# Moving the projection of the embeddings to the start of a two-block kernel on one Trainium2 core

## The chip, the core and the metric

The kernel runs on one core of one Trainium2 chip, as one program. The metric is device time in microseconds (us); less is better. Five engines work side by side, each through its own list of instructions in order: PE (matrix products), ACT (ScalarE), DVE (VectorE), POOL (GpSimd) and SP, which here only issues transfers. Two instructions on different engines are ordered by semaphores alone. The order on each engine is fixed when the program is built: the kernel writes it out by hand.

## What is computed

Two transformer blocks, one after the other, on 256 rows of 1024 numbers in float32. The first is modulated by a condition `c`; the second adds, at its very end, a gated projection of per-row embeddings `p`:

```python
x = x + g1 * (mixed @ w_out)                    # end of the first block's attention
h2 = rms(x, ln2_g) * (1 + sc2) + sh2            # its second norm
x = x + g2 * ((silu(h2 @ w_gate) * (h2 @ w_up)) @ w_down)
...                                             # second block: mixers, feed forward
gate = sigmoid(rms_norm(x, norm_ple_g) @ w_ple_gate)
x = x + gate * (p @ w_ple_proj)                 # p: 256 x 256, w_ple_proj: 256 x 1024
return rms_norm(x, norm_final_g)
```

The product `p @ w_ple_proj` depends on no other result. It may be computed at any time before the last step.

## The kernel before, in words

Rows are cut into two tiles of 128 (`t` = 0, 1). Every weight arrives as a unit of 128 x 2048 float32 (1.05 MB; the units `ko` are 128 x 1536). ACT rounds a unit to `wh`, DVE subtracts to get the rest `wl` (`split`, L281), and each product is made of three matmuls (`mm3`, L449): high by high, low by high, high by low. `_order()` (L50) lists the units in the order in which SP loads them and in which they are split. `load_to` (L265) issues the loads: a unit lies in one of three `raw` buffers (the modulation weights `a1` in slabs of 128 x 1024 instead), and up to four split units (`wh`, `wl`) are alive at a time.

The start, up to L629, is written out by hand. SP issues `pf`, then `a1` unit 0, `x`, `ko` unit 0, and further units (L424 to L432). PE passes its time with dummy products on a tile of ones (`keep_warm`, L552, counts in `WARM`). Then comes `a1` unit 0 (L530: four products on PE, four column scalings on DVE, sum `r`), the sum of squares of both row tiles on ACT (`sumsq`, L514), the reciprocal root on POOL (`rsqrt`, L458), the scaled rows `xn`, their transposes, and `modulate` and `modulate2` (L576, L592), which give the first normed tile `h1b`. From L605 a loop over eight steps multiplies by `ko`: in each step 18 matmuls `pa`, the next `a1` unit and the next modulation.

From L1122 on a planner decides the order: a model of the engines' clocks (`Pace`) is carried along while the program is built, side tasks (`run`) are advanced in `tick` (L396) when the model holds their inputs ready, and `until` (L410) lets the model's PE clock run on while nothing is ready. It sets the order of instructions, not their times on the chip.

The projection of the embeddings is such a side task. `ple_prep` (L1145) loads `p` transposed (tile `pT`, 128 x 512) through POOL's queue and splits it. `ple_proj` (L1153) makes, for each row tile and each half of the columns, six matmuls of 512 columns into `ppa` and copies them by ACT to `ppo`; POOL's queue writes `ppo` to a buffer `pp` in HBM, from where it is read back at the very end (L1688). Its unit `("pp",)` stands behind the units of the first output projection `wo1`, and the condition `spare` (L1295) lets it run only once `wo1` is issued and the planner is idle: that is while the residual and the norm `n2` behind `wo1` (`norm_shift`, L1230, `shift_steps`, L1250) are being worked out for the feed forward step `up`.

Of the kernel before, what the change touches and what calls it, by code (L numbers as in the profile page):

```python
# [10 lines left out]
F32 = mybir.dt.float32  # L11
F32R = mybir.dt.float32r
# [36 lines left out]

def _order():  # L50

    o = [("a1", 0)]
    for j in range(KT):
        o.append(("ko", j))
        if j + 1 < KT:
            o.append(("a1", j + 1))
    ad = lambda s: [("ad", s, q, h) for q in range(2) for h in range(2)]
    m = [(n, u) for n in ("dk", "fv", "dv") for u in range(2)] + [("wo1", h, cb) for h in range(2) for cb in range(2)]
    m.append(("pp",))
    a = ad(0) + ad(1) + ad(2)  # L60
    for i, p in reversed(list(enumerate(ORDER))):
        m[p:p] = a[2 * i:2 * i + 2]
    o += m

    def ffn(n, nb, nd):
        gu = lambda b: [("g" + n, b, 0), ("g" + n, b, 1)]
        dn = lambda b: [("d" + n, b, h) for h in range(nd)]
        r = gu(0) + gu(1)
        for b in range(2, nb):
            r += dn(b - 2) + gu(b)  # L70
        return r + dn(nb - 2) + dn(nb - 1)
    f = ffn("1", NB1, 1)
    for i, k in enumerate(ad(3)):
        f.insert(12 + 4 * i, k)
    o += f
    for hf in range(2):
        for n in ("v", "q", "k"):
            o += [(n, hf, 0), (n, hf, 1)]
    for n in ("zv", "zu", "ga", "gb"):
        for hf in range(2):  # L80
            o += [(n, hf, 0), (n, hf, 1)]
    o += [("wo2", h, cb) for h in range(2) for cb in range(2)]
    o += ffn("2", NB2, 2)
    o += [("pg", hf, h) for hf in range(2) for h in range(2)]
    return o
# [3 lines left out]

A1_FIRST, WARM = True, (20, 4, 4, 2)

ON_DVE = ()
ORDER = (3, 6, 6, 8, 9, 11)
# [111 lines left out]
def body(ctx, tc, ins, out):  # L207
# [20 lines left out]
    def psB(name):  # L228
        if st["paced"]:
            bfree.sort()  # L230
            clock["PE"] = max(clock["PE"], bfree.pop(0))
        return ps.tile([P, 512], F32, tag="B", name=name)
# [4 lines left out]
    def slab(name, dt=F32):  # L237
        return sb.tile([P, 1024], dt, tag="s", bufs=12, name=name)

    def half(name, dt=F32):  # L240
        return sb.tile([P, 512], dt, tag="w", bufs=11, name=name)
# [23 lines left out]
    def load_to(n):  # L265
        while st["dma"] < min(n, len(order)):
            i = st["dma"]
            if order[i][0] == "a1":
                raws[i] = [slab(f"raw{i}{g}") for g in range(2)]
                for g in (1, 0):  # L270
                    Q.dma_start(raws[i][g], src[i][0][:, g * 1024:(g + 1) * 1024])
            else:
                raw = sb.tile([P, 2048], F32, tag="raw", bufs=NRAW, name=f"raw{i}")
                ring.append(raw.tensor.name)
                if len(ring) > NRAW:
                    clock["DMA"] = max(clock["DMA"], pace.last.get(ring[-1 - NRAW], 0.0))
                Q.dma_start(raw[:, :src[i][1]], src[i][0])
                raws[i] = raw
            st["dma"] += 1

# [8 lines left out]
    def process():  # L289

        i, k = st["proc"], order[st["proc"]]
        if st["part"] == 0:
            st["parts"] = par(HALVES) if st["paced"] and not pe_only() else 1
        n, c = st["parts"], st["part"]
        w = src[i][1] // n
        if k[0] in ("a1", "ad"):
            handlers[k[0]](k, raws[i], c)
        else:
            if c == 0:
                assert len(live) < NSP, (k, live)  # L300
                parts[k] = [sb.tile([P, 2048], F32R, tag=q, bufs=NSP, name=f"{q}{i}") for q in ("wh", "wl")]
                live.append(k)
            if st["first"]:
                for a in range(0, w, 512):
                    split(*parts[k], raws[i], a, a + 512)
                    if a == 0:
                        st["first"]()
            else:
                split(*parts[k], raws[i], c * w, (c + 1) * w)
        st["part"] += 1  # L310
        if st["part"] == n:
            raws.pop(i)
            st["part"] = 0
            st["proc"] += 1
            load_to(st["proc"] + (NRAW + 2 if st["proc"] < 13 else NRAW))

    def can_process():
        if st["proc"] == len(order):
# [6 lines left out]
    def use(k, ahead=False, h=1, first=None):  # L325
        st["first"] = first
        while place[k] > st["proc"] or (place[k] == st["proc"] and st["part"] <= h):
            process()
        if not ahead:
            st["used"] = max(st["used"], place[k])  # L330
        return parts[k]
# [20 lines left out]
    def on(*aps, slack=None):  # L352
        return lambda: pace.when(*aps) <= clock["PE"] + (par(SLACK) if slack is None else slack)
# [5 lines left out]
    def slot(n=1):  # L359
        return lambda: sum(f <= clock["PE"] + par(SLACK) for f in bfree) >= n  # L360

    def flag(*names):
        return lambda: all(n in flags for n in names)
# [58 lines left out]

    pf = sb.tile([P, PF_W], F32, name="pf")
    Q.dma_start(pf, ins["pf"])  # L424
    if A1_FIRST:
        load_to(1)
    x = []
    for t in range(NT):
        xt = sb.tile([P, D], F32, name=f"x{t}")
        Q.dma_start(xt, ins["x"][t * P:(t + 1) * P, :])  # L430
        x.append(xt)
    load_to(NRAW)  # L432
    pc = sb.tile([P, PC_W], F32, name="pc")
    bias_t = sb.tile([P, 4096], F32, tag="bias", name="bias1")
    al = bias_t[:, 0:1280].rearrange("p (h k) -> p h k", k=256)
# [13 lines left out]
    def mm3(acc, a, b, start, stop):  # L449
        (ah, al_), (bh, bl) = a, b  # L450
        T.matmul(acc, lhsT=ah, rhs=bh, start=start, stop=False)
        T.matmul(acc, lhsT=al_, rhs=bh, start=False, stop=False)
        T.matmul(acc, lhsT=ah, rhs=bl, start=False, stop=stop)
# [98 lines left out]
    def keep_warm(n):  # L552
        for _ in range(n):
            T.matmul(warm[:, 0:P], lhsT=ones, rhs=ones, start=True, stop=True)

    keep_warm(WARM[0])
    xn1, rx = [], []
    if A1_FIRST:
        process()
    for t in range(NT):  # L560
        ss = sumsq(x[t], f"n1{t}")
        rx.append(rsqrt(ss, 1, 1.0 / D, f"n1{t}"))
        xn1.append(slab(f"xn1{t}"))
    if not A1_FIRST:
        process()
    keep_warm(WARM[1])

    def scale_x(t, a, b):
# [36 lines left out]
    for j in range(KT):  # L605
        wh, wl = use(("ko", j))
        for p in range(3):
            for cb in range(3):
                c = slice(cb * 512, cb * 512 + 512)
                for t in range(NT):  # L610
                    T.matmul(accs[cb][t], lhsT=hT[t][p // 2][:, j, :], rhs=(wh, wl, wh)[p][:, c],
                             start=j == 0 and p == 0, stop=j == KT - 1 and p == 2)
            if p == 0 and j + 1 < KT:
                process()
            if p == 1 and j + 1 < KT:
                modulate(j + 1)
                use(("ko", j + 1))
                modulate2(j + 1)
            if p == 0 and j + 1 == KT:
                use(("dk", 0), True)  # L620
            if p == 0 and j + 1 == KT:
                V.tensor_copy(fgh, pcs("fgw"))
                V.tensor_tensor(fgl, pcs("fgw"), fgh.bitcast(F32), op=ALU.subtract)
        live.remove(("ko", j))
        if j == 4:
            Q.dma_start(pc, ins["pc"])
        if j == 6:
            Q.dma_start(bias_t[:, 0:1280], ins["alibi"])
    use(("dk", 1), True)  # L629


# [506 lines left out]
    proj(("dv",), keep(lambda t: vv[t][:, 512:1024], "dv"))  # L1138


    pp = dr.tile([NT, P, D], F32, name="pp")
    pTh = half("pTh", F32R)
    pTl = half("pTl", F32R)

    def ple_prep():  # L1145
        pT = half("pT")
        G.dma_start(pT, ins["p2T"])
        yield on(pT)
        V.tensor_copy(pTh, pT)
        V.tensor_tensor(pTl, pT, pTh.bitcast(F32), op=ALU.subtract)  # L1150
        flags.add("pT")

    def ple_proj():  # L1153
        for t in range(NT):
            o_ = slab(f"ppo{t}")
            for cb in range(2):
                yield flag("pT"), lambda: ("pp",) in parts, spare, slot()
                acc = psB(f"ppa{t}{cb}")
                wh, wl = use(("pp",))
                for k in range(2):  # L1160
                    o = k * 1024 + cb * 512
                    a = slice(k * 256 + t * P, k * 256 + t * P + P)
                    mm3(acc, (pTh[:, a], pTl[:, a]), (wh[:, o:o + 512], wl[:, o:o + 512]), k == 0, k == 1)
                yield on(acc)
                S.activation(o_[:, cb * 512:(cb + 1) * 512], acc, AF.Copy)
                free(acc)
            G.dma_start(pp[t], o_)
        done(("pp",))


    def out_proj(name, mTs, mflag, fin):
        acc = {}
        for h in range(2):
# [118 lines left out]

        until(flag(f"{nflag}{t}{u}"), on(hTn[t][0][:, 4 * u:4 * u + 4, :], hTn[t][1][:, 4 * u:4 * u + 4, :]))

    def spare():  # L1295
        return st["idle"] and "wo1" in flags

    run(ple_prep())
    run(ple_proj(), 2)
    hT_n, *hT_all = hT_tiles("n2")  # L1300
    out_proj("wo1", mT, "mT", residual(0, norm_shift("n2", hT_n, "n2")))
    hT = hT_n
# [598 lines left out]
```

## Time and profile before

| | |
|---|---|
| three runs | 786.50, 786.51, 786.88 us (median 786.51) |
| the profiled execution, its own time | 787.08 us |
| its span, first to last instruction | 785.3 us |
| PE busy | 770.6 us, 98% of the span |
| DVE, ACT, POOL busy | 66%, 54%, 4% of the span |
| HBM read and written | 156.8 MB and 2.1 MB, 202 GB/s over the span |
| granted TensorE clock, mean | 0.998 |

Times within the trace count from the first instruction. A row of the time line gives start, duration, engine, line, operation, output and inputs, and in brackets how long the engine stood idle before and what it waited for. Every instruction bears L153, the line of the helper that records them; tiles are told apart by name. PEld is the loading of PE's stationary operand. A matmul's duration contains the drain, so successive matmuls overlap; their rate is read from start to start.

### The profile page before, as it was taken

The page shows a single profiled execution, that of the slowest core. Times are in us where ns is not written, and L with a number is a line of the kernel's source. Part 1 is how long each engine was busy: PE and PEld are TensorE (multiplying, and loading weights), DVE is VectorE, ACT ScalarE, POOL GpSimd, SP SyncE. Part 2 cuts the span into 40 slices and gives each one's busy share as a digit, 9 for nine tenths or more (in the row PEclk, how much of TensorE's full clock was granted, in tenths as well). Part 3 has the DMA queues.
Part 4 walks back from the last instruction along what each step waited for, and adds up shares of the span by engine and source line. Part 5 has one row for each costly group of instructions (what it writes and reads, how often), then busy time and mean ns, then how long its engine had stood idle before and what let it go on. Part 6 is the DMA issues. An engine that isn't in the chain of part 4 may idle for free.

```text
span 785.3 us, 10687 instructions
## 1 busy us (share of the span) xinstructions
PE 770.6 (98%) x4110; PEld 631.6 (80%) x4110; DVE 520.4 (66%) x913; ACT 424.9 (54%) x711; POOL 34.4 (4%) x73
## 2 busy tenths in 40 slices
PE   8999999999999999999999999999999999999996
PEld 7777667778888888888879878888888888888885
DVE  4878867667576866558674658746676665566583
ACT  4457467466554554456556584554475455445463
POOL 0000000121100000001100001000010000000011
PEclk9999999999999999999999999999999999999999
DMA  8967853755855666534762334545555544554331
GB/s 338 413 245 300 291 192 126 285 220 193 321 214 215 240 230 227 199 124 159 297 214 68 148 108 161 215 167 209 187 174 203 190 162 184 214 214 183 138 108 54
DMA packets 25251, 159.61 MB, mean 203 GB/s; under 512 B 2944, under 2 KB 3104, under 8 KB 8816
## 3 DMA queue, kind: packets, MB, share of 16 engines
q1 hardware_dynamic: 23184, 152.27, 52.0%
q0 software_dynamic: 2016, 6.66, 2.5%
q8 instruction: 32, 0.52, 0.3%
q14 instruction: 19, 0.16, 0.1%
HBM read 156.80 MB, written 2.12 MB: 202 GB/s over the span
## 4 chain that ended last, share of the span: by engine, by line
PE 91%; ACT 3%; DVE 3%; issue 1%; DMA 1%; POOL 0%; SPq 0%; POOLq 0%; ACTq 0%; DVEq 0%
PE up L153 27%; PE dn L153 19%; PE wo L153 5%; PE pa L153 3%; PE pga L153 3%; PE gb L153 3%; PE ga L153 3%; PE zu L153 3%; PE v L153 2%; PE zv L153 2%; PE dk L153 1%; PE k0T L153 1%; PE q0T L153 1%; PE q1T L153 1%; PE ap L153 1%; PE k1T L153 1%
## 5 line engine op out<-in xcount | busy, mean ns | idle before, releaser
L153 DVE TENSOR_TENSOR wl<-raw,wh 128x1024 fp32r<-128x1024 f32 (+3 forms) x218 | 278.7, 1309 | 109.0 <-ACT wh L153 108.9
L153 ACT ACTIVATE wh<-raw 128x1024 fp32r<-128x1024 f32 (+3 forms) x218 | 235.8, 1124 | 66.2 <-PE up L153 14.2
L153 PE MATMUL up<-n2b,wh 128*128 128x512 f32 x320 | 114.4, 401 | 0.0
L153 PE MATMUL up<-n2b,wl 128*128 128x256 f32 x320 | 89.8, 281 | 0.0
L153 PE MATMUL dn<-wh,aTh 128*128 128x512 f32 x216 | 84.9, 393 | 0.0
L153 PE MATMUL dn<-wl,aTh 128*128 128x512 f32 x216 | 84.3, 390 | 0.0
L153 PE MATMUL dn<-wh,aTl 128*128 128x512 f32 x216 | 84.1, 390 | 0.0
L153 PE MATMUL up<-n4b,wh 128*128 128x512 f32 x224 | 79.5, 399 | 0.0
L153 PEld LDWEIGHTS up<-n2b,wh 128*128 128x128 f32 x320 | 60.1, 188 | 15.6 <-issue 1.1
L153 ACT ACTIVATE fs<-up 128x256 f32<-128x256 f32 x68 | 25.9, 381 | 83.9 <-PE up L153 83.9
L153 PE MATMUL up<-n4b,wl 128*128 128x256 f32 x224 | 62.9, 281 | 0.0
L153 PEld LDWEIGHTS up<-n2b,wl 128*128 128x128 f32 x320 | 60.4, 189 | 1.0 <-issue 0.5
L153 DVE TENSOR_TENSOR fs<-up,fs 128x256 f32<-128x256 f32 x68 | 28.7, 422 | 39.7 <-ACT fs L153 39.5
L153 PEld LDWEIGHTS up<-n4b,wh 128*128 128x128 f32 x224 | 42.1, 188 | 10.3
L153 PEld LDWEIGHTS dn<-wl,aTh 128*128 128x128 f32 x216 | 40.6, 188 | 8.9
L153 PEld LDWEIGHTS dn<-wh,aTh 128*128 128x128 f32 x216 | 40.6, 188 | 8.5
L153 PEld LDWEIGHTS dn<-wh,aTl 128*128 128x128 f32 x216 | 40.6, 188 | 7.9
L153 PEld LDWEIGHTS up<-n4b,wl 128*128 128x128 f32 x224 | 42.3, 189 | 0.3
L153 ACT ACTIVATE aTh<-fs 128x512 fp32r<-128x512 f32 x24 | 15.2, 632 | 37.4 <-DVE fs L153 37.4
L153 DVE TENSOR_TENSOR aTl<-fs,aTh 128x512 fp32r<-128x512 f32 x24 | 16.6, 693 | 16.6 <-ACT aTh L153 16.5
L153 PE MATMUL pa<-wh,h1b 128*128 128x512 f32 x96 | 24.5, 400 | 0.8 <-ACT h1b L153 0.6
L153 PE MATMUL v<-wh,n3b 128*128 128x512 f32 x64 | 20.9, 405 | 0.6 <-DVE n3b L153 0.6
(686 smaller groups left out, 1393.5 us busy)
## 6 DMA issues: line engine op xcount, KB each, us to landing
raw<-in_ws_dram SPq DMA_DIRECT2D x112, 1024.0 KB, 4.8
raw<-in_ada_dram SPq DMA_DIRECT2D x16, 1024.0 KB, 5.0
raw<-in_ada_dram SPq DMA_DIRECT2D x16, 512.0 KB, 10.9
raw<-in_wko_dram SPq DMA_DIRECT2D x8, 768.0 KB, 9.6
bias<-rd POOLq DMA_DIRECT2D x1, 2048.0 KB, 10.7
x<-in_x_dram SPq DMA_DIRECT2D x2, 512.0 KB, 7.2
pp<-ppo POOLq DMA_DIRECT2D x2, 512.0 KB, 3.6
ppt<-pp POOLq DMA_DIRECT2D x2, 512.0 KB, 3.9
```

The lines of the kernel that those rows point to most:

```text
L153: r = f(*a, **k)
```

## The change

The unit `("pp",)` becomes the first of the order. `p` transposed and this unit (in two halves, one transfer each) are loaded right behind `pf`; then `x`; then the modulation and `ko` units. The products are issued behind the first dummy products and ahead of `a1` unit 0, in four accumulators at once, the four copies by ACT stand ahead of the two sums of squares, and the two writes to HBM are issued by POOL in the text behind the `ko` loop. The side tasks are gone from behind `wo1`.

```diff
-    o = [("a1", 0)]
+    o = [("pp",), ("a1", 0)]
...
-    m.append(("pp",))
...
-                Q.dma_start(raw[:, :src[i][1]], src[i][0])
+                w = 1024 if order[i][0] == "pp" else src[i][1]
+                for a in range(0, src[i][1], w):
+                    Q.dma_start(raw[:, a:a + w], src[i][0][:, a:a + w])
...
-            load_to(st["proc"] + (NRAW + 2 if st["proc"] < 13 else NRAW))
+            load_to(st["proc"] + (NRAW + 2 if st["proc"] < 14 else NRAW))
...
-    if A1_FIRST:
-        load_to(1)
+    pT = half("pT")
+    Q.dma_start(pT, ins["p2T"])
+    load_to(1)
     x = []
     for t in range(NT):
         xt = sb.tile([P, D], F32, name=f"x{t}")
         Q.dma_start(xt, ins["x"][t * P:(t + 1) * P, :])
         x.append(xt)
-    load_to(NRAW)
+    load_to(NRAW + 1)
...
     keep_warm(WARM[0])
+
+    pp = dr.tile([NT, P, D], F32, name="pp")
+    pTh = half("pTh", F32R)
+    pTl = half("pTl", F32R)
+    V.tensor_copy(pTh, pT)
+    V.tensor_tensor(pTl, pT, pTh.bitcast(F32), op=ALU.subtract)
+    wh, wl = use(("pp",), first=lambda: None)
+    ppo = [slab(f"ppo{t}") for t in range(NT)]
+    ppa = [[psA(f"ppa{t}{cb}") for cb in range(2)] for t in range(NT)]
+    for k in range(2):
+        for cb in range(2):
+            o = k * 1024 + cb * 512
+            for t in range(NT):
+                a = slice(k * 256 + t * P, k * 256 + t * P + P)
+                mm3(ppa[t][cb], (pTh[:, a], pTl[:, a]), (wh[:, o:o + 512], wl[:, o:o + 512]), k == 0, k == 1)
+    done(("pp",))
     xn1, rx = [], []
-    if A1_FIRST:
-        process()
+    process()
+    for t in range(NT):
+        for cb in range(2):
+            S.activation(ppo[t][:, cb * 512:(cb + 1) * 512], ppa[t][cb], AF.Copy)
     for t in range(NT):
         ss = sumsq(x[t], f"n1{t}")
...
+    for t in range(NT):
+        G.dma_start(pp[t], ppo[t])
     use(("dk", 1), True)
...
-    def ple_proj():
-        for t in range(NT):
-            o_ = slab(f"ppo{t}")
-            for cb in range(2):
-                yield flag("pT"), lambda: ("pp",) in parts, spare, slot()
...
-    run(ple_prep())
-    run(ple_proj(), 2)
```

## Rows read from the trace of the kernel before

**Rows 1.** The page, part 4: shares of the chain that ended last, by engine.

```profile
PE 91%; ACT 3%; DVE 3%; issue 1%; DMA 1%; POOL 0%; SPq 0%; POOLq 0%; ACTq 0%; DVEq 0%
```

**Rows 2.** Busy us by window: PE, PEld, DVE, ACT, POOL, granted clock, DMA share, GB/s.

```profile
5.00:10.00 5.00, 5.00 (x40) 4.47 (x39) 2.23 (x5) 1.06 (x2) 0.00 (x0) 1.00 1.02 417
20.00:30.00 10.00, 10.00 (x60) 7.13 (x58) 8.19 (x16) 4.73 (x6) 0.45 (x1) 1.00 1.02 414
```

**Rows 3.** Time line, the first 14 us: start, duration, engine, operation, [idle before].

```profile
1.04 7.48 PE L153 MATMUL warm<-ones 128*128 128x128 f32 x40 [1.04 <-DVE ones L153]
...
6.37 0.35 DVE L153 TENSOR_SCALAR r<-raw,cond 128x256 f32<-128x256 f32 x1 [3.21 <-DMA raw<-in_ada_dram]
...
8.94 1.06 ACT L153 ACTIVATE n10j<-x 128x1024 f32<-128x1024 f32 x1 [6.06 <-DMA x<-in_x_dram]
...
10.21 1.06 ACT L153 ACTIVATE n11j<-x 128x1024 f32<-128x1024 f32 x1
...
12.11 0.63 ACT L153 ACTIVATE wh<-raw 128x512 fp32r<-128x512 f32 x1 [0.74 <-DMA raw<-in_wko_dram]
...
13.41 0.56 ACT L153 ACTIVATE h1b<-pt,sh,sc 128x256 fp32r<-128x256 f32 x1 [0.68 <-DVE sc L153]
...
14.03 0.74 PE L153 MATMUL pa<-wh,h1b 128*128 128x512 f32 x2 [0.59 <-ACT h1b L153]
```

**Rows 4.** Time line, two steps of the loop over `ko`.

```profile
22.11 0.64 PE L153 MATMUL ap<-raw,condz 128*32 128x256 f32 x8
...
22.60 1.49 ACT L153 ACTIVATE wh<-raw 128x1536 fp32r<-128x1536 f32 x1 [1.87 <-DMA raw<-in_wko_dram]
...
27.68 0.64 PE L153 MATMUL ap<-raw,condz 128*32 128x256 f32 x8
```

**Rows 5.** By tile, `ppa` and `pT`: count, duration min/median/max, first and last start.

```profile
L153 PE MATMUL ppa<-wh,pTh x8: 389/389/499, 166.3 to 172.9; 128*128 128x512 f32 x8
...
L153 ACT ACTIVATE ppo<-ppa x4: 575/588/594, 170.1 to 176.0; 128x512 f32<-128x512 f32 x4
...
L153 DVE CAST pTh<-pT x1: 416/416/416, 146.6 to 146.6; 128x512 fp32r<-128x512 f32 x1
```

**Rows 6.** Time line behind the output projection `wo1`, PE only.

```profile
166.32 0.39 PE L153 MATMUL ppa<-wh,pTh 128*128 128x512 f32 x1
...
168.82 0.39 PE L153 MATMUL ppa<-wl,pTh 128*128 128x512 f32 x1
...
169.65 1.27 PE L153 MATMUL n2t<-pf,n2x 128*128 128x128 f32 x8 [0.45 <-ACT n2x L153]
...
173.37 0.39 PE L153 MATMUL ppa<-wl,pTh 128*128 128x512 f32 x1
```

**Rows 7.** The chain of waits in order of time: start, duration, what it spent.

```profile
160.61 3.02 issue
163.63 0.10 ACT wh L153
163.72 1.73 issue
165.45 0.71 ACT n2j L153 x2
...
170.21 0.92 ACT ppo L153 x2
...
173.84 0.49 ACT ppo L153
...
176.26 7.53 PE up L153 x33
```

**Rows 8.** Time line, the last matmul of the kernel.

```profile
777.24 0.28 PE L153 MATMUL pga<-wl,n5b 128*128 128x256 f32 x1
```

**Rows 9.** By window, columns as in rows 2: the dummy products, and the end.

```profile
1.00:7.00 6.00, 5.96 (x28) 5.96 (x29) 1.10 (x5) 1.21 (x2) 0.00 (x0) 1.00 0.82 255
7.00:8.00 1.00, 1.00 (x11) 1.00 (x10) 0.93 (x3) 0.00 (x0) 0.00 (x0) 1.00 1.01 414
...
782.00:783.00 1.00, 0.00 (x0) 0.00 (x0) 0.00 (x0) 0.00 (x0) 0.00 (x0) 0.50 0.92 348
```

More of the change, by code (lines that the diff above doesn't have):

```diff
@@ L85, in _order @@
     return o
-A1_FIRST, WARM = True, (20, 4, 4, 2)
+WARM = (20, 4, 4, 2)
 ON_DVE = ()
@@ L563, in body @@
         xn1.append(slab(f"xn1{t}"))
-    if not A1_FIRST:
-        process()
     keep_warm(WARM[1])
@@ L1138, in body @@
     proj(("dv",), keep(lambda t: vv[t][:, 512:1024], "dv"))
[L1141 to L1151, printed above, removed]
-    def ple_proj():
-        for t in range(NT):
-            o_ = slab(f"ppo{t}")
-            for cb in range(2):
-                yield flag("pT"), lambda: ("pp",) in parts, spare, slot()
[L1158 to L1168, printed above, removed]
     def out_proj(name, mTs, mflag, fin):
@@ L1293, in halves @@
         until(flag(f"{nflag}{t}{u}"), on(hTn[t][0][:, 4 * u:4 * u + 4, :], hTn[t][1][:, 4 * u:4 * u + 4, :]))
-    def spare():
-        return st["idle"] and "wo1" in flags
-    run(ple_prep())
-    run(ple_proj(), 2)
     hT_n, *hT_all = hT_tiles("n2")
```

## The prediction

> **What bounds the kernel now.** I read four views, in this order. First the shares of the chain that ended last: 91% of it is PE [rows 1], so only what delays PE, or what PE waits for, moves the time. The question is then where PE works on the embeddings' projection now, where it will, and what PE would have done at either place. Second, the time line behind the output projection `wo1` [rows 6] with the chain of waits there [rows 7]: the projection's matmuls start at 166.32 and the last starts at 173.37, but none of them is in the chain. The chain of that stretch runs over ACT: a weight split that waits 3.02 us, the sums of squares `n2j` behind it, and the copies `ppo` (0.92 and 0.49 us), until PE takes `up` without a break from 176.26. So PE fills with the projection a stretch in which it would have to wait anyway. Third, the time line of the first 14 us [rows 3]: PE runs dummy products until 8.52, and the first real matmul `pa` starts at 14.03; its path is x landing, `n10j` at 8.94, `n11j` at 10.21, the roots, the transposes, `h1b` at 13.41. Fourth, the DMA of that stretch: it moves 417 and 414 GB/s at a full share [rows 2], so the start is bounded by bytes and by that path together, while the loop behind it repeats every 27.68 - 22.11 = 5.57 us on PE [rows 4].
>
> **The change, part by part.** The sum is made on the profiled execution: span 785.3, own time 787.08, that is 1.78 us outside the span, which the change doesn't touch. Its own time lies 0.57 us above the median 786.51; I take the difference found and put it on the median.
>
> *The load.* `pT` (128 x 512 x 4 bytes = 0.26 MB) and the unit (1.05 MB) go ahead of all but `pf`: 1.31 MB at 0.417 MB per us [rows 2] = 3.1 us later for every `a1` and `ko` unit. Behind the loop's beginning this is hidden if PE is at least as late (below). x comes ahead of `a1` unit 0 now: ahead of it stand 1.31 MB more and 1.05 MB less, so it lands 0.6 us later than 8.94, at about 9.6; `a1`'s first half, used at 6.37 before [rows 3], has 2.36 MB more ahead of it and comes 5.7 us later, at 12.0.
>
> *The products at the start.* 24 matmuls. From 166.32 to 168.82 eleven intervals take 2.50 us [rows 6], 0.227 us each; 24 of them take 5.45 us, the last one's result standing 0.16 us later than that (its duration is 0.39 [rows 5]). They start when the dummy products end, 8.52, if the first half of the unit has been split by then. Its bytes are `pf`, `pT` and 0.52 MB, 0.26 MB more than `pf` and the first half of `a1` had, which was used at 6.37: so it lands at 7.0, its first quarter is rounded by 7.7 (0.63 us for 128 x 512 [rows 3]), and there is 0.8 us of slack; `pTh` takes 0.42 us [rows 5] before that. So PE ends them at 8.52 + 5.45 + 0.16 = 14.1. Bounds: no later unless the halves land over 0.8 us late; I allow 1.5 us upward, nothing downward, since the number of dummy products stays.
>
> *The copies.* Four on ACT, 0.588 us long [rows 5]; three can follow the accumulators as they finish, the last waits for the last matmul at 14.1, and as the two copies of [rows 7] hold the chain 0.46 us each and more for the first, the next ACT instruction starts some 0.55 us behind: 14.7. That next instruction is `n10j`. Here is the point: in the text the copies stand ahead of the sums of squares, ACT keeps its order, so x, landed at 9.6, waits until 14.7. `n10j` moves from 8.94 to 14.7, by 5.75 us, and the path from it to `pa`, 14.03 - 8.94 = 5.09 us, is unchanged: `a1` unit 0 (12.0, four DVE steps and the sum, about 15 with its products on PE behind the projection's) and `ko` unit 0 (12.11 + 3.1 = 15.2, when ACT is busy with `n11j` until 17.2) both come in time. First `pa`: 14.03 + 5.75 = 19.8. Everything that PE does from there on is 5.75 us later.
>
> *Does the loop stay PE's?* Its loads come 3.1 us later and their consumers 5.75 us, so they gain 2.65 us of margin. Against it stand the two writes of `ppo`, 1.05 MB: POOL has nothing of length between the roots and these writes, so it issues them at about 18 us, into the full DMA: 2.5 us at 0.417 MB per us. The margin covers them. Without it the cost would be up to 2.5 us, since ACT waited 1.87 us for one `ko` unit already [rows 4]; I take 0 and keep 0 to 1.
>
> *What is removed behind `wo1`.* The 24 matmuls leave a hole rather than a gain: the chain there [rows 7] has no `ppa`. What leaves the chain are the copies: 0.92 + 0.49 = 1.4 us. The split with its wait of 3.02 us stays as I read the planner: four split units are alive, so the next split needs the release of `wo1`'s third unit whichever unit it is, and it is emitted at the same point, ahead of `n2j`. A unit is loaded and split one place sooner, but PE doesn't wait for splits in this stretch. Next late behind the copies is the same ACT chain, and at the second tile's transposes PE. Bounds of this gain: 1.4 up to 3.5 (if `n2j` also comes ahead of the split of 163.63 to 165.45 [rows 7]). I take 1.4.
>
> *The rest.* `pT`'s load on POOL's queue at 140, two DVE steps at 147, one split of some 2 us on either engine at 149 leave stretches in which PE is full; that work was hidden, and is worth 0 (its cover is PE's own work, and the planner may order its neighbours a little differently: plus or minus 0.5).
>
> Sum: +5.75 - 1.4 = +4.35 us. 786.51 + 4.35 = 790.9.
>
> **A rule against the trace.** In the hole PE has, from its last `wo` matmul at about 166.5, only eight transposes at 169.65 and three matmuls until about 175. At the end of the kernel the clock reads 0.50 in the window 782 to 783, the lower of the two levels (1.2 against 2.4 GHz), after the last matmul ended at 777.52 [rows 8, 9]; and 28 dummy products took the first 6 us while 11 took the next one [rows 9], so beginning from rest PE is slower too, though the column reads 1.00 there. The Trainium skill, "TensorE: Matmul & The Clock Gate", section "Why this matters for your kernels", warns of idle gaps between bursts of matmuls, since one brings the clock back to its lower level; by it the removed filler would have been what kept the clock up. The trace before has no such hole to test it; this is the second rival.
>
> **The rivals.**
>
> 1. *The hole closes, not slower.* If the planner, without the unit, puts the split elsewhere and `n2j` comes as x is ready, PE could go from `wo` to `up` with no wait. It would gain the 5.45 us and the waits that are there already (0.45 us at 169.65 and a few tenths more [rows 6]), about 6.2 us; against +5.75 that is 786.1. It decides at one place: the first `n2t` must start at 166.6 instead of 169.65, so 3 us must leave the chain ahead of it, and of those only the split's 1.8 us are in sight [rows 7]. With the start at its lower bound, the bytes' 3.1 us alone, it would be 783.4; for that the copies would have to stand behind the sums of squares, and they don't. With half of it (3.5 us gained) it is 788.8.
>
> 2. *The clock falls in the hole, slower still.* `up`'s 512-column matmuls then cost 0.45 instead of 0.227 us until the clock rises. At the start that took until about 7.0, 6 us of matmuls [rows 9]; at half rate that loses up to 3 us, some of which the norm of the second row tile would have spent waiting anyhow. I take 2: 792.9, up to 794.
>
> 3. *The start pays only its bytes.* If ACT's copies delay nothing, the start moves by 3.1 and the end is 786.51 + 3.1 - 1.4 = 788.2. Against it: the order in the text.
>
> **How the numbers follow.** Forecast 0.50 (790.9, with its own range of 789.6 to 792.4: the start's 1.5 us upward, the planner's 0.5, a further gain behind `wo1`); the clock 0.23 (791.5 to 794); the hole half closed or the bytes alone 0.16 (788.2 to 789.5); the hole closed 0.11 (783.4 to 787). The range reaches from 788.0 to 794.0; what it leaves out is the closed hole and a start later than my bounds. A measurement of this kernel tells about 0.2%, 1.6 us, from no change: faster is below 784.9, same up to 788.1. Of the closed hole half is faster, half the same; some of the third rival is the same: faster 0.06, same 0.08, slower 0.86.
>
> **What would show it.** In the profile after: `ppa` from about 8.5 to 14; `n10j` at about 14.7 behind a copy and not behind x; first `pa` at about 19.8; the loop's step still 5.57 us; `wo`'s last matmul 5.75 us later than before; then a stretch of some 6 us in which PE is nearly idle, with the split still ahead of `n2j`, and `up` without a break from about 176.26 + 4.35 = 180.6. The granted clock by window in that stretch decides the second rival. The forecast is wrong if `pa` starts before 18 or after 21.5, if the split has left its place, or if the loop waits for its units.

## The result, and the profile after

The changed kernel takes 795.0 us (median; 794.96 to 795.16), the kernel before 786.5: a ratio of 1.0108 with a 95% interval of 1.009 to 1.0125, slower. The forecast was 790.9 with a range of 788.0 to 794.0: the direction held, the size didn't, and the time lies 1.0 us above the range. The profiled execution has a span of 793.2 us and an own time of 795.0, which is the median; that of before was 787.08, 0.57 above its median. So of the 8.5 us between the medians the two traces show 7.9.

In all rows of this and the next section times count from the first instruction, and a row of the time line gives start, duration, engine, line, operation, output and inputs, and in brackets the idle time before it and what ended that.

The start, time line of the kernel after (compare [rows 3]):

```profile
12.23 0.35 DVE L152 TENSOR_SCALAR r<-raw,cond 128x256 f32<-128x256 f32 x1 [1.85 <-DMA raw<-in_ada_dram]
...
13.18 1.58 ACT L152 ACTIVATE ppo<-ppa 128x512 f32<-128x512 f32 x3 [0.76 <-PE ppa L152]
...
13.43 0.39 PE L152 MATMUL ppa<-wl,pTh 128*128 128x512 f32 x1
...
14.62 1.07 ACT L152 ACTIVATE n10j<-x 128x1024 f32<-128x1024 f32 x1
...
17.69 1.31 POOL L152 DMA_DIRECT2D pp<-ppo  x2
...
19.48 0.73 PE L152 MATMUL pa<-wh,h1b 128*128 128x512 f32 x2 [0.59 <-ACT h1b L152]
```

This is the forecast almost to the tenth: the projection ends at 13.43 + 0.39 = 13.8 (14.1 forecast), `n10j` follows a copy without a wait at 14.62 (14.7), `a1`'s first half is used at 12.23 (12.0), and the first `pa` starts at 19.48 (19.8), 5.45 us later than before.

The loop by window (busy us of PE, PEld, DVE, ACT, POOL, granted clock, DMA share, GB/s; compare [rows 2]):

```profile
20.00:30.00 10.00, 9.69 (x56) 6.46 (x55) 8.21 (x17) 6.67 (x8) 0.00 (x0) 1.00 1.02 418
```

And on the time line, the first matmuls of two steps (compare [rows 4]):

```profile
27.53 0.64 PE L152 MATMUL ap<-raw,condz 128*32 128x256 f32 x8
33.09 0.64 PE L152 MATMUL ap<-raw,condz 128*32 128x256 f32 x8
```

The step is 33.09 - 27.53 = 5.56 us (5.57 before): the margin did cover the two writes of `ppo`, which POOL issued at 17.69 into a full DMA. PE stays late and takes its last `wo` matmul at 172.05, 5.95 us later than before (166.10 in the trace of before; 5.75 was forecast). So far the sum holds.

Behind `wo1` it doesn't. The chain of waits of the kernel after, in order of time (compare [rows 7]):

```profile
159.95 9.56 PE wo L152 x42
...
169.53 1.93 ACT wh L152
...
171.48 2.29 DVE wl L152
173.77 0.61 DVE rg L152
...
174.41 0.69 DVE x L152
175.10 0.65 DVE full L152 x2
...
178.52 3.23 PE up L152 x6
```

A split is in the chain again, but at another place. Before, ACT's `wh` stood ahead of `n2j` [rows 7]. Now both `n2j` of the first row tile come first, and the split behind them delays by its DVE half, `wl`, all that DVE still owes the norm: the last residual (`rg`, `x`) and `full`. The time line shows the order, and PE's part (compare [rows 6]):

```profile
167.03 0.63 ACT L152 ACTIVATE n2j<-x 128x512 f32<-128x512 f32 x1 [3.75 <-DVE x L152]
...
168.55 0.63 ACT L152 ACTIVATE n2j<-x 128x512 f32<-128x512 f32 x1 [0.79 <-DVE x L152]
...
169.53 1.92 ACT L152 ACTIVATE wh<-raw 128x2048 fp32r<-128x2048 f32 x1 [0.26 <-PE wo L152]
...
172.05 0.39 PE L152 MATMUL wo<-wl,mTh 128*128 128x512 f32 x1
172.28 1.10 PE L152 MATMUL n2t<-pf,n2x 128*128 128x128 f32 x8
...
175.83 1.50 ACT L152 ACTIVATE full<-n2t,sh,sc 128x128 f32<-128x128 f32 x4 [2.55 <-DVE full L152]
...
178.52 1.52 PE L152 MATMUL up<-wh,n2b 128*128 128x512 f32 x2 [5.13 <-ACT n2b L152]
...
181.54 1.91 PE L152 MATMUL n2t<-pf,n2x 128*128 128x128 f32 x8
...
185.58 0.72 DVE L152 TENSOR_SCALAR full<-n2t,sc,sh 128x128 f32<-128x128 f32 x2
...
191.02 0.44 PE L152 MATMUL at<-pf,sg 128*128 128x128 f32 x2 [1.13 <-DVE sg L152]
...
194.74 0.39 PE L152 MATMUL up<-n2b,wh 128*128 128x512 f32 x1
```

And the same places in the kernel before:

```profile
166.10 0.39 PE L153 MATMUL wo<-wl,mTh 128*128 128x512 f32 x1
...
173.60 0.83 PE L153 MATMUL up<-wh,n2b 128*128 128x512 f32 x2
...
186.62 0.39 PE L153 MATMUL up<-n2b,wh 128*128 128x512 f32 x1
```

The first transposes `n2t` follow the last `wo` matmul with no gap, 3.3 us sooner than before if both are counted from that matmul (172.28 - 172.05 = 0.2, before 169.65 - 166.10 = 3.55). But then PE is idle for 5.13 us, and what follows is slow: two `up` matmuls take 1.52 us here (0.83 before), the eight transposes of the second row tile 1.91 us (1.27 before [rows 6]). The granted clock says why (by window, columns as above):

```profile
177.00:178.00 1.00, 0.00 (x0) 0.00 (x0) 0.00 (x0) 1.00 (x4) 0.00 (x0) 0.56 0.82 344
178.00:183.00 5.00, 4.48 (x13) 3.46 (x14) 1.66 (x4) 2.31 (x4) 2.96 (x6) 0.50 0.08 15
...
184.00:185.00 1.00, 1.00 (x6) 0.78 (x6) 0.03 (x1) 0.90 (x2) 0.00 (x0) 1.00 0.00 0
```

The clock falls within the window 177 to 178 to 0.50, the lower of the two levels (1.2 against 2.4 GHz), so that `up` begins at it, and it is back at about 184: the second rival of the prediction.

One measure tells all runs of this study apart: the stretch from the start of the last `wo` matmul to the first matmul of `up`'s second half (`up<-n2b,wh`). It is 186.62 - 166.10 = 20.52 us before and 194.74 - 172.05 = 22.69 us after. The projection's 5.45 us have left the stretch, and it has become 2.2 us longer; the forecast had it 1.4 us shorter.

The loss doesn't lie ahead of `up`, though. Its first matmul starts 178.52 - 172.05 = 6.47 us behind the last `wo` matmul, and before it was 173.60 - 166.10 = 7.50. From there to the first matmul of the second half it takes 16.22 us, against 13.02 before. In these 16.22 us lie the slow matmuls, and the norm of the second row tile, which comes late: two of DVE's `full` steps for it start only at 185.58, and PE waits 1.13 us ahead of `at` at 191.02, the transposes of `sg`, the first result that comes out of `up`.

### The profile page after: what moved, and what is told of

It reads as the page before. It is cut to its first block, busy times and chain, and to the rows that moved or that the text cites. A ratio compares the mean times of both kernels' runs of the same rounds, so it can differ in the third digit from the quotient of the medians.

```text
span 793.2 us, 10703 instructions
## 1 busy us (share of the span) xinstructions
PE 772.8 (97%) x4110; PEld 633.2 (80%) x4110; DVE 521.1 (66%) x915; ACT 425.3 (54%) x713; POOL 32.5 (4%) x72
## 4 chain that ended last, share of the span: by engine, by line
PE 91%; ACT 4%; DVE 3%; issue 1%; POOL 0%; POOLq 0%; ACTq 0%; DVEq 0%
PE up L152 26%; PE dn L152 19%; PE wo L152 5%; PE pa L152 3%; PE pga L152 3%; PE gb L152 3%; PE ga L152 3%; PE zu L152 3%; PE v L152 2%; PE zv L152 2%; PE dk L152 1%; PE k0T L152 1%; PE q0T L152 1%; PE q1T L152 1%; PE ap L152 1%; PE k1T L152 1%
```

## The experiments

Ratios are to the kernel before, timed on the same chip (786.9 us). The kernel before took 0.4 us less beside the changed kernel (786.5), and the changed kernel wasn't timed again with the experiments, so a median's difference from its 795.0 us is known to some tenths only. Two theories stand against each other at first: that the forecast was right in kind, with the start dearer than it looked, or that the start costs what was forecast and the emptied stretch costs time instead of giving it back.

**The start alone.** The kernel after, with the projection computed a second time at its old place, from the unit loaded again (`pq`):

```diff
+    m.append(("pq",))
     a = ad(0) + ad(1) + ad(2)
...
+    run(ple_prep())
+    run(ple_proj(), 2)
```

> The changed kernel with the projection computed a second time where it stood before (a further unit behind wo1, its own tiles, its result written to a buffer that nobody reads): the start is the new one, the stretch behind wo1 has its filler again. Theory (two separate costs: the start 5.5 us, the emptied stretch behind wo1 some 3 us): 792.0 us, first pa at 19.5, the order behind wo1 and the clock there as in the kernel before. Rival (the start only costs its bytes, or its delay is taken up later, and the rest comes from behind wo1): 786.5 to 790. Rival (the delay of the start itself disturbs what follows): 795.

Measured: 792.45 us, ratio 1.0071 (1.0056 to 1.0086). The first `pa` starts at 19.35, and behind `wo1` ACT keeps the order of before, the split ahead of both `n2j`:

```profile
168.99 1.92 ACT L153 ACTIVATE wh<-raw 128x2048 fp32r<-128x2048 f32 x1 [3.02 <-issue]
170.81 0.61 ACT L153 ACTIVATE n2j<-x 128x512 f32<-128x512 f32 x1
```

The stretch is 191.96 - 171.46 = 20.50 us, that of before. So the start costs 5.5 us, close to the 5.75 of the sum, and nothing of it is given back on the way.

**The hole alone.** The kernel before, with the projection taken out altogether; rows of x stand in for its result in the last step, so the output is another:

```diff
-    m.append(("pp",))
...
-    run(ple_prep())
-    run(ple_proj(), 2)
...
-        G.dma_start(ppt[t], pp[t])
+        G.dma_start(ppt[t], ins["x"][t * P:(t + 1) * P, :])
```

> The kernel before without the projection of the embeddings at all: no unit, no 24 matmuls, no copies, no writes; at the very end x's input rows stand in for its result, so the output is another. Start as before. Theory: slower although it does less, 789.4 us: the stretch behind wo1 takes 3 us longer, with the split behind the sums of squares and the granted clock at 0.5 for some 6 us. My prediction's step (the copies leave the chain, nothing else changes): 785.1. Rival (the new order behind wo1 comes from the start, not from the missing filler): 785 to 786.5 with the order as before.

Measured: 788.88 us, ratio 1.0028 (1.0016 to 1.0039). A kernel with 24 matmuls, a unit of 1.05 MB and four copies less is slower. Its time line behind `wo1`:

```profile
163.47 1.92 ACT L152 ACTIVATE wh<-raw 128x2048 fp32r<-128x2048 f32 x1 [0.26 <-PE wo L152]
...
166.22 1.10 PE L152 MATMUL n2t<-pf,n2x 128*128 128x128 f32 x8
...
172.47 1.52 PE L152 MATMUL up<-wh,n2b 128*128 128x512 f32 x2 [5.14 <-ACT n2b L152]
...
184.65 0.44 PE L152 MATMUL at<-pf,sg 128*128 128x128 f32 x2 [1.84 <-DVE sg L152]
```

And by window:

```profile
172.00:173.00 1.00, 0.54 (x1) 0.29 (x1) 0.56 (x1) 0.93 (x2) 0.83 (x3) 0.68 0.00 0
173.00:175.00 2.00, 2.00 (x5) 1.49 (x5) 0.74 (x2) 1.34 (x2) 2.00 (x4) 0.50 0.05 9
...
185.00:186.00 1.00, 1.00 (x6) 0.82 (x6) 0.88 (x1) 0.88 (x3) 0.00 (x0) 1.00 0.00 0
186.00:187.00 1.00, 1.00 (x4) 0.71 (x3) 0.99 (x3) 1.00 (x2) 0.00 (x0) 0.50 0.00 0
...
189.00:190.00 1.00, 1.00 (x5) 0.78 (x5) 0.05 (x1) 0.00 (x0) 0.00 (x0) 0.79 0.97 410
```

Up to about 182 it is the picture of the kernel after, 5.9 us sooner: the `wh` that waited for the release of `wo1`'s third unit (0.26 us), the same 5.1 us of idle PE, the same lower clock. Then the clock falls a second time, at 186, behind PE's wait of 1.84 us ahead of `at`, and is back only in the window 189 to 190; so the stretch is 189.97 - 165.99 = 23.98 us here, 1.3 more than in the kernel after. This is the slowest of the six executions of this kernel (789.87 us); whether the clock fell twice in the others isn't known. With the start as it was, the order has changed too, so it is the missing unit that changes it and not the start. In the medians the hole costs 2.0 us. Start and hole make 5.5 + 2.0 = 7.5 us, and 1.0071 x 1.0028 = 1.0099 lies within the interval of the whole change.

Two causes are left for the hole: the clock, and the place of the split.

**The clock.** The kernel after, with 20 dummy products issued on PE ahead of the first `up`, in an accumulator that `up` clears afterwards. They are float32, so each is two passes:

```diff
                 halves(nflag, hT, t, u)
+                if n == "1" and t == u == 0:
+                    for _ in range(20):
+                        nc.tensor.matmul(pu[:, 0:P], lhsT=ones, rhs=ones, start=True, stop=True)
```

> The changed kernel with 20 dummy products of 128 x 128 on PE (40 passes) behind the first norm's transposes and ahead of up; they are kept from the planner, so the order of all else stays. Theory (the fallen clock costs about 2 us of the 8.5): granted clock 1.0 through the stretch, up's first six matmuls 0.23 apart instead of 0.44, 793.0 us. Rival (ACT's chain alone sets when up goes on, the clock is free): 795.0.

Measured: 793.93 us, ratio 1.0087 (1.0071 to 1.0104). On the time line:

```profile
173.48 4.63 PE L1318 MATMUL up<-ones 128*128 128x128 f32 x40
...
178.78 0.50 PE L152 MATMUL up<-wh,n2b 128*128 128x512 f32 x1 [0.67 <-ACT n2b L152]
```

And by window:

```profile
178.00:183.00 5.00, 4.10 (x21) 3.02 (x21) 2.02 (x4) 3.33 (x8) 2.96 (x6) 1.00 0.09 25
```

The clock stays at 1.00, but `up` still starts 6.47 us behind the last `wo` matmul (172.31 in this trace), as in the kernel after: its wait was never for PE. The stretch is 193.55 - 172.31 = 21.24 us, 1.45 less than after; the median falls by 1.1 us, though the intervals of the two ratios overlap, so the size rests on the trace. That is the clock's part, less than the 2 us taken for it, and not the larger part of the hole's surprise.

**The split.** The kernel after, with one condition more in the planner's first loop: while a residual or a norm of the first block is under way (`hot`), that loop doesn't split ahead:

```diff
-        while can_process() and ahead() < par(LEAD) and (ahead() < 1 or raw_here()):
+        while can_process() and ahead() < par(LEAD) and (ahead() < 1 or raw_here()) and not (st["hot"] and st["phase"] == 0):
```

> The changed kernel with one condition more in the planner: while wo1's residual and norm are under way it splits no further unit. Theory (the split on ACT and DVE ahead of the norm's steps is part of the 3 us behind wo1): DVE's last residual follows wo at once instead of behind 2.29 us of wl, up's first matmul 1 to 2 us sooner, the clock falls all the same; 793.5 us. Rival (POOL's root of the second row tile and the clock set when up goes on, the split is covered): 795.0.

Measured: 792.63 us, ratio 1.0073 (1.006 to 1.0086), more than was expected of it:

```profile
173.61 1.36 DVE L152 TENSOR_SCALAR full<-n2t,sc,sh 128x128 f32<-128x128 f32 x4
...
177.11 0.49 PE L152 MATMUL up<-wh,n2b 128*128 128x512 f32 x1 [4.00 <-ACT n2b L152]
...
181.69 1.36 DVE L152 TENSOR_SCALAR full<-n2t,sc,sh 128x128 f32<-128x128 f32 x4
```

DVE reaches `full` at 173.61 instead of 175.01, and `up` starts 177.11 - 171.84 = 5.27 us behind the last `wo` matmul instead of 6.47. The stretch is 191.38 - 171.84 = 19.54 us, one less than before the change and near the forecast's 20.5 - 1.4 = 19.1. So holding the split back is worth 3.15 us of the stretch and 2.4 us in the medians: the larger part. Of the 3.15 us 1.2 lie ahead of `up`, where the trace of the kernel after shows `wl` in the way. The other 1.95 lie behind it, and there the condition changes more than the place of one split: DVE makes all four `full` steps of the second row tile in one go at 181.69, and PE's wait ahead of `at` is gone. The split's two halves and this second change weren't tried apart. The clock still falls here, at about 178.5, after `up` has begun, so that a part of its price may be saved here too.

**The split in the kernel before.** The same line, in before.

> The kernel before with the same condition: no split while wo1's residual and norm are under way, the projection still behind wo1. Theory (the chain there begins with the split that waits 3.02 us, and PE is covered by the projection): n2j of the first row tile at 163.4 instead of 165.45, up without a break from 174.6 instead of 176.26; 785.0 us, faster than both. Rival (the unit that is held back is then late for up): 786.5 or more.

Measured: 791.02 us, ratio 1.005 (1.0039 to 1.0062). A miss. `n2j` and `up` come sooner, as expected, but the unit held back is one that `up` itself needs a little later:

```profile
172.72 0.41 PE L153 MATMUL up<-wh,n2b 128*128 128x512 f32 x1
...
181.28 0.73 PE L153 MATMUL up<-wh,n2b 128*128 128x512 f32 x2 [2.32 <-ACT wh L153]
...
182.54 0.50 PE L153 MATMUL up<-wl,n2b 128*128 128x512 f32 x1 [0.53 <-DVE wl L153]
```

PE waits 2.32 us for its `wh` and 0.53 us for its `wl`, about the 2.9 us by which this execution (789.81 us) is longer than the kernel before. So the split that stood in the chain of before was work that had to be done about there. In the kernel after no unit of the projection stands between `wo1`'s units and `up`'s, so that, by the order in the code, the splits are one unit further on; `up` ran there without waiting for the one held back.

**The copies.** The kernel after, with the four copies `ppo` behind both sums of squares:

```diff
-    for t in range(NT):
-        for cb in range(2):
-            S.activation(ppo[t][:, cb * 512:(cb + 1) * 512], ppa[t][cb], AF.Copy)
     for t in range(NT):
         ss = sumsq(x[t], f"n1{t}")
...
+    for t in range(NT):
+        for cb in range(2):
+            S.activation(ppo[t][:, cb * 512:(cb + 1) * 512], ppa[t][cb], AF.Copy)
```

> The changed kernel with the four copies of the projection behind the two sums of squares on ACT instead of ahead of them. Theory (the copies hold the path at the start): n10j at about 9.7 when x has landed; then the modulation unit, whose first half is used at 12.2, and the projection on PE until 13.8 are last, first pa at 18.0 to 18.4 instead of 19.5, 793.7 us. Rival (the path at the start is the bytes' and PE's, not the copies'): pa stays at 19.5, 795.0.

Measured: 793.54 us, ratio 1.0085 (1.007 to 1.01).

```profile
9.91 1.06 ACT L152 ACTIVATE n10j<-x 128x1024 f32<-128x1024 f32 x1
...
18.27 0.73 PE L152 MATMUL pa<-wh,h1b 128*128 128x512 f32 x2 [0.59 <-ACT h1b L152]
```

Between the two, DVE and PE:

```profile
12.47 0.35 DVE L152 TENSOR_SCALAR r<-raw,cond 128x256 f32<-128x256 f32 x1 [1.87 <-DMA raw<-in_ada_dram]
...
15.24 0.28 DVE L152 TENSOR_SCALAR xn<-x,n11y 128x128 f32<-128x128 f32 x1
...
16.07 1.06 PE L152 MATMUL warm<-ones 128*128 128x128 f32 x8
16.97 0.27 PE L152 MATMUL pt<-pf,xn 128*128 128x128 f32 x1
```

`n10j` starts 4.7 us sooner, and `pa` only 1.2 us. Next late is the path of `a1`, whose first half is used 12.47 - 6.37 = 6.1 us later than before [rows 3]: on DVE the rows of x are scaled behind the sum `r`, and the second row tile, ready at 15.5, is transposed only at 16.97, behind eight passes of the dummy products that the code puts between the two transposes. That these were free before and are in the way here wasn't tried by itself.

**All three.** The kernel after with the copies behind, the splits held and the dummy products.

> The changed kernel with all three remedies: copies behind the sums of squares, no split during wo1's norm, 20 dummy products in the stretch behind wo1. Theory (three separate costs): 1.3 + 1.5 + 1.1 us less than the changed kernel, 791.1 us; what is left, over 4 us above the kernel before, is the projection's bytes and matmuls at the start with nothing gained behind wo1. Rival (they cover one another): 792.5 or more.

Measured: 790.4 us, ratio 1.0044 (1.0029 to 1.0058).

The stretch is 190.44 - 171.03 = 19.41 us, with the clock at 1.00 throughout. With the split held the clock is worth hardly more there (19.54 without the dummies). With the clock up, as in the run with the dummy products alone, holding the split is worth 21.24 - 19.41 = 1.83 us. The order of the copies doesn't touch the stretch: alone it left it at 193.47 - 170.78 = 22.69 us. Alone the three edits gave 1.5, 2.4 and 1.1 us in the medians, 4.9 together before rounding; here they give 4.6. No kernel of this study beats the kernel before: the start still costs 18.42 - 14.03 = 4.4 us, and the emptied stretch gives back 1.1. Even at the 3.1 us that the 1.31 MB alone would take at the start by the prediction's estimate, the sum would stay some 2 us above it.

## Why the prediction was wrong, step by step

- *What bounds the kernel.* Right. The chain is PE's by 91% before and after; what the change moved is what PE waits for.
- *The load, the products, the copies.* Right, each within 0.4 us: 13.8 for 14.1, 14.62 for 14.7, 19.48 for 19.8. The start alone measured 5.5 us for 5.75.
- *The loop stays PE's, the writes are covered.* Right: 5.56 us per step.
- *The next split "is emitted at the same point, ahead of `n2j`".* This is the step that failed, and with it the term of -1.4 us that supposes it: the stretch measured 22.69 us where the forecast had 19.1. I saw that the wait for the release of `wo1`'s third unit would stay whichever unit came next, and it did: `wh` starts at 163.63 before, at 169.53 after, 2.5 us ahead of the last `wo` matmul in both. What I took as fixed was which instruction the planner emits ahead of it. The planner emits what its model holds ready; with one unit less it emitted both `n2j` first. On ACT that was a gain, the 3.3 us by which `n2t` came sooner. On DVE, which I hadn't followed, `wl` kept its place and its 2.29 us ahead of the last residual, and `full` stands behind both, so of the 3.3 us only 1.0 reached `up`'s first matmul. Behind that the steps of the second row tile came late, and PE paid for them at the lower clock and in the wait ahead of `at`. I named this case as the upper bound of the gain (up to 3.5 us); I followed only one of the two engines on which a split runs. That the order changes because the unit is gone is shown by the hole alone and the start alone, and that it costs something besides the clock by the two runs with the dummy products (21.24 us with the split in its place, 19.41 with it held, the clock at 1.00 in both). Why the planner's model comes to that order no run shows.
- *What leaves the chain: 1.4 us.* Found up to `up`'s first matmul (1.0 us) and lost behind it in the kernel after (+2.2 in the whole stretch), and nearly found where the two disturbances are taken away: 20.52 - 19.41 = 1.1 us.
- *The second rival.* It happened, at half the price: 1.1 us measured in the medians (1.45 in the stretch) for 2 taken. It alone would have given 792.0, within my range. The forecast had treated the idle stretch as certain and the falling clock as a rival with 0.23; the trace of before showed the clock at 0.50 some 4.5 us after the last matmul [rows 8, 9], and some six us of a nearly idle PE were what I forecast. The two steps together made the likeliest case, and I hadn't put them together.
- *The median.* 0.57 us of the miss is none of the mechanism: the profiled execution of before lay that much above its median, so a difference of the traces (7.9) is smaller than that of the medians (8.5).

The sum with measured terms, on the traces: 5.45 to the first `pa`, 0.5 more up to the last `wo`, 2.2 in the stretch, -0.1 to the end: 8.0, by the last matmul, which starts at 785.27 instead of 777.24 [rows 8].

The Trainium skill, "TensorE: Matmul & The Clock Gate", section "Why this matters for your kernels", was right against my sum: the gap brought the clock down. What it was worth here, though, was the smaller part.

## What to carry to other kernels

Work that fills a stretch in which the critical engine waits anyway is free only there. Moved to a start bound by bytes it cost 5.5 us here, about its full length, and the emptied place gave back 1.1 us at best. Where a planner orders the work, taking a unit out can move the decisions behind it: follow the next few instructions on all engines that share the moved step, here DVE's half of a split and not ACT's alone. Before filler is taken out, add up how long PE will then be idle, and count the slower matmuls behind the gap as part of the forecast.

## What the runs showed of the hardware

The clock's fall isn't tied to one distance from the last matmul. In the kernel after the last transpose ended at 172.28 + 1.10 = 173.38, and the clock fell within the window 177 to 178; in the hole alone it ended at 166.22 + 1.10 = 167.32, and the fall lies in the window 172 to 173, so at least 4.7 us behind. It came back while PE worked at the lower level: in the kernel after at about 184, 5.4 us after `up` had begun.

A shorter pause can go either way. In the hole alone PE paused for 1.84 us ahead of `at` at 184.65, and the clock was at 0.50 from 186 on, when PE had been at work again for 1.3 us. With the dummy products PE paused for 1.72 us at the same place, and with the splits held in the kernel before for 2.32 us in the middle of `up`; in both traces the clock stayed at 1.00 behind the pause. Of the six executions of the last of these kernels two have a mean granted clock of 0.998 and take 789.2 and 789.8 us, the other four 0.991 to 0.994 and 790.9 to 792.8 us. Its spread, 3.7 us, is wider than that of any other kernel here, and goes with the clock; which pause brought it down in the longer ones no trace here shows.
